# A hybrid decoder step on one Trainium2 core: the sample groups' score and value products, their PSUM banks, and the second layer of the cache compression

## The chip, the cores and the metric

The kernel runs on one core of one Trainium2 chip, as one launch. The metric is the device time of that core in microseconds. TensorE multiplies matrices into PSUM banks of 512 float32 columns; VectorE, ScalarE and GpSimd work beside it; SyncE and GpSimd issue most of the DMAs.

## The reference, cut to what matters

One inference step of a two-layer decoder, for a prompt of 512 tokens and for 8 samples of one token, each with a cache of 2048 positions in 16 pages. The change lies in the sparse attention of the samples:

```python
h = jax.nn.gelu(h_a[:, :-1] + h_b[:, 1:] + h_pe)      # compression, first layer
kc, vc = h @ w2                                        # second layer, for keys and for values
kc = partial_rope(kc, c_end)                           # rotates the first 16 of 64 key dims
p_c = masked_softmax(q . kc);  o_c = p_c @ vc          # compressed branch
_, idx = lax.top_k(importance(p_c), 16)                # 16 of 33 blocks of 64 positions
o_s = softmax(q . ks[idx]) @ vs[idx]                   # selected branch
o_w = softmax(q . kw) @ vw                             # last 512 positions
o = g0 * o_c + g1 * o_s + g2 * o_w
```

## The kernel before, in words

Every layer runs a feed-forward network, a mixer (`mid`) and another feed-forward network; the changed lines are in `mid`. There the 8 samples' compressed cache is computed by one generator (`compress_cache`, samples b = 0 to 7), and the attention of the samples by four others (`samples`, groups g = 0 to 3 of two samples each). `weave` takes the instructions of both by turns; group 3 is woven with the prompt's attention instead. The program is then put in order by a planner, which goes by priorities in the order of the text and by its own costs: when the next instruction of an engine is not ready by its reckoning, a later one that is ready goes first. On the chip each engine follows the order so found, and waits where something is late.

A bank is taken with `bank(pool)`. The pools are opened with `reuse_waits="tile"`: a tile's first writer waits until the readers of the bank's earlier tile are done. The pools are `saM` (one bank, `M`: a group's small products), `saS` (two banks: scores `S` and outputs `O`), `saT` (transposes), `ctp` (one bank, `pa`: second layer of the compression).

The group's products have few rows. A group's 128 rows are four quarters of 32 (two halves z of the cache, two samples j), and each quarter is a product of its own with 32 columns of weights that writes its own 32 partitions. L1189 makes the selected scores, two banks of 512 columns, four quarters each; the pages stand in `G[z, j]`, four tiles of 1 MB from the pool `sag` (four buffers), of which GpSimd gathers three pages each (L1118) and SyncE loads five (L1122). L1198 and L1199 make the window scores and the scores of the sample's own key, L1249 and L1258 the values of the selected pages and of the window, L1262 and L1263 the values of the sample's own row (8 rows of weights), L1264 the compressed branch (127 rows). `fetch_sel` for the group after stands behind L1249, so its DMAs wait for the buffers that L1249 reads. A float32 product shows in the trace as two weight loads and two matmuls (two passes), so counts there are twice those of the text.

In the compression, L708 makes the first layer (with the high and low parts of input and weights), `prepare` (L693 on ScalarE, L694 on VectorE) its inputs a step ahead, L730 the gelu, and `second` the second layer: the keys twice, with `w2` and with its rotated copy `w2r` (L736, and L738 for the prompt in sample 0), the values at L740, then the rotation on VectorE (L742 to L744) and a copy on ScalarE (L745). VectorE's L1192 adds the mask to the scores; the mask comes from the small products L1149 to L1178.

Of the kernel before, what the change touches and what calls it, by code (L numbers as in the profile page):

```python
# [7 lines left out]
F32 = mybir.dt.float32  # L8
# [3 lines left out]
OP = mybir.AluOpType  # L12
# [110 lines left out]
class Trunk:  # L123
# [376 lines left out]
    def mid(self, l):  # L500
        nc, I = self.nc, self.I
# [3 lines left out]
        a = self.pool(att, "att", side="right")  # L505
# [10 lines left out]
        self.w2 = a.tile([128, 2, 64], F32, name="w2")  # L516
        self.w2r = a.tile([128, 64], F32, name="w2r")
        self.hpe = a.tile([128, 2], F32, name="hpe")
# [125 lines left out]
    def compress_start(self, l, p):  # L644

        nc, I = self.nc, self.I
        self.w1 = []
        pet = p.tile([128, 2, 2, 8], F32, name="pet")
        for i in range(2):
            raw = self.rawp.tile([128, 8, 256], F32, name="raw")  # L650
            w = raw.rearrange("p k (z h) -> p (k z) h", h=128)
            nc.sync.dma_start(w, I[("nsa_phi_k1", "nsa_phi_v1")[i]][l].rearrange("(q p) h -> p q h", p=128))
            nc.sync.dma_start(self.w2[:, i], I[("nsa_phi_k2", "nsa_phi_v2")[i]][l])
            nc.sync.dma_start(pet[:, i], I[("nsa_pe_k", "nsa_pe_v")[i]][l].rearrange("p (z q) -> p z q", z=2))
            self.lo = nc.gpsimd
            with self.tc.issue_after(self.queries.ins):
                self.w1.append([self.split(w[:, 8 * z:8 * z + 8]) for z in range(2)])
            self.lo = nc.vector
        nc.vector.memset(self.w2r, 0.0)
        nc.vector.tensor_scalar(self.w2r[:, 0:8], self.w2[:, 0, 8:16], -1.0, None, op0=OP.mult)  # L660
        nc.vector.tensor_copy(self.w2r[:, 8:16], self.w2[:, 0, 0:8])
        return p, pet

    def compress_cache(self, l, p, kcv, cx, G, start):

        nc = self.nc
# [45 lines left out]
        def second(b, acc):  # L712
# [6 lines left out]
            hp = []  # L719
# [12 lines left out]
            pa = self.bank(self.ctp)  # L732
            for j, w in enumerate((self.w2[:, 0], self.w2r)):
                for kv in range(2):
                    r = slice(kv * 64, kv * 64 + 64)
                    nc.tensor.matmul(pa[r, j * 128:j * 128 + 128], w, h[:, kv, :], start=True, stop=True)  # L736
                    if b == 0:
                        nc.tensor.matmul(pa[r, 384 + j * 32:416 + j * 32], w, hp[0][:, 0, kv], start=True, stop=True)  # L738
            for kv in range(2):
                nc.tensor.matmul(pa[:, 256 + kv * 64:256 + kv * 64 + 64], h[:, 2 + kv, :], self.w2[:, 1], start=True, stop=True)  # L740
            t = p.tile([128, 128], F32, name="kct")
            nc.vector.tensor_mul(t, pa[:, 128:256], self.C["kc_sin"])  # L742
            nc.vector.tensor_mul(kcT, pa[:, :128], self.C["kc_cos"])
            nc.vector.tensor_add(kcT, kcT, t)  # L744
            nc.scalar.activation(vc, pa[:, 256:384], AF.Copy)  # L745
            if b == 0:
                t = p0.tile([128, 32], F32, name="pt1")
                nc.vector.tensor_mul(t, pa[:, 416:448], self.C["kc_sin"][:, :32])
                nc.gpsimd.memset(self.kcp, 0.0)
                for kv in range(2):  # L750
                    r = slice(kv * 64, kv * 64 + 64)
                    nc.vector.tensor_mul(self.kcp[r, kv], pa[r, 384:416], self.C["kc_cos"][r, :32])
                    nc.vector.tensor_add(self.kcp[r, kv], self.kcp[r, kv], t[r])
# [370 lines left out]
    def fetch_win(self, l, pw, g):  # L1124
        for j in range(2):
            w = pw.tile([128, 1024], F32, name="W")
            self.nc.sync.dma_start(w, self.I["winT"][l, 2 * g + j])
            self.sgq[g]["w", j] = w

    def samples(self, l, g, p, pg, pw):  # L1130

        nc = self.nc
        G = self.sgq[g]
        QB, kcT, vc = self.QB, self.kcT, self.vc
        M = self.bank(self.saM)

# [49 lines left out]
        for c in range(2):  # L1186
            S = self.bank(self.saS)
            for z, j, r in quarters:
# [4 lines left out]
                                    msk[:, 8 * c:8 * c + 8, None].to_broadcast([128, 8, 64]), op=OP.add)  # L1193
        S = self.bank(self.saS)
        for j in range(2):
            for z in range(2):
                r = 64 * z + 32 * j
                nc.tensor.matmul(S[r:r + 32, :256], QB[:, 2 * g + j], G["w", j][:, 256 * z:256 * z + 256], start=True, stop=True)  # L1198
            nc.tensor.matmul(S[32 * j:32 * j + 32, 256:258], QB[:, 2 * g + j], self.kTs[:, :, 2 * g + j], start=True, stop=True)  # L1199
# [45 lines left out]

        O = self.bank(self.saS)
        for c in range(8):
# [12 lines left out]
        for j in range(2):  # L1260
            own, o = slice(32 * j, 32 * j + 32), slice(64 + 32 * j, 96 + 32 * j)
            nc.tensor.matmul(O[own, :128], sT[:, own], self.srows[:, 128:256], start=False, stop=True, skip_group_check=True)  # L1262
            nc.tensor.matmul(O[own, 128:256], sT[:, o], self.srows[:, 384:512], start=False, stop=True, skip_group_check=True)  # L1263
            nc.tensor.matmul(O[own, 256:384], pc[:, own], vc[:127, j], start=False, stop=True, skip_group_check=True)  # L1264
        yield 900.0
        if g < 3:
# [688 lines left out]
```

## Time and profile before

| | us |
|---|---|
| median of 3 runs (lowest, highest) | 3108.46 (3104.69, 3116.01) |
| the profiled execution, by the device | 3104.94 |
| its span from first to last instruction | 3103.2 |
| TensorE busy, share of the span | 3028.1, 98% |
| VectorE busy | 1598.7, 52% |
| ScalarE busy | 1120.1, 36% |
| GpSimd busy | 536.1, 17% |
| mean granted TensorE clock | 0.987 of full |

Busy times overlap; a matmul's time includes its way through the array, so neighbours overlap as well, and the distance from one start to the next is what counts for TensorE. In timelines, a line is a run of equal instructions (their number behind the x), its start, its length, and in brackets the idle time of the engine before it with what ended it.

### The profile page before, as it was taken

To read this page: it belongs to the slowest core of one execution; us is meant where nothing else is said; L and a number is where in the kernel's file an instruction comes from. 1 tells how busy PE (TensorE), PEld (TensorE's weight loads), DVE (VectorE), ACT (ScalarE), POOL (GpSimd) and SP (SyncE) were. 2 spreads that over 40 slices of the span, in tenths; PEclk is the share of its full clock that TensorE was granted. 3 is DMA by queue.
4 is the path that set the end of the run, shared out by engine and by line. 5 is a ranking of instruction groups with operands and counts; after the bars stand their busy time and mean duration, and the time that the engine had idled before them with its cause. 6 is when DMAs were issued, how large, how long until landed. Compare 5 with 4: busy or idle time off the path is not lost. (4 is left out here: it accounts for less than half of the span.)

```text
span 3103.2 us, 62136 instructions
## 1 busy us (share of the span) xinstructions
PE 3028.1 (98%) x25364; PEld 2906.8 (94%) x25364; DVE 1598.7 (52%) x3586; ACT 1120.1 (36%) x2226; POOL 536.1 (17%) x809
## 2 busy tenths in 40 slices
PE   8999999999999999999999999999999999999998
PEld 8999998777999999999999999887789999999998
DVE  7633356566655365333496333565666453743334
ACT  4332235456224233232233222354652242333322
POOL 2611031321001021001147010213210010210010
PEclk9999999999999999999999999999999999999999
DMA  5543254632553232232234332547234433223221
GB/s 159 198 148 133 89 159 134 209 96 63 156 138 103 88 101 91 82 99 86 82 121 169 96 103 76 172 124 218 83 93 140 122 98 102 89 82 103 89 87 64
DMA packets 358630, 360.17 MB, mean 116 GB/s; under 512 B 40068, under 2 KB 341668, under 8 KB 358216
## 3 DMA queue, kind: packets, MB, share of 16 engines
q1 hardware_dynamic: 342584, 333.58, 34.4%
q0 software_dynamic: 7440, 20.00, 2.2%
q8 instruction: 199, 3.26, 0.4%
q10 hardware_dynamic: 8320, 2.62, 0.4%
q14 instruction: 87, 0.71, 0.1%
HBM read 332.48 MB, written 36.28 MB: 119 GB/s over the span
## 5 line engine op out<-in xcount | busy, mean ns | idle before, releaser
L239 PE MATMUL ps<-xh,whi 128*128 128x264 f32 (+1 forms) x4448 | 1257.6, 285 | 14.1 <-ACT whi L228 6.1
L240 PE MATMUL ps<-xl,whi 128*128 128x264 f32 (+1 forms) x4448 | 1257.4, 284 | 2.0 <-DVE xl L323 2.0
L241 PE MATMUL ps<-xh,wlo 128*128 128x264 f32 (+1 forms) x4448 | 1254.1, 283 | 2.4 <-DVE wlo L229 2.4
L229 DVE TENSOR_TENSOR wlo<-raw,whi 128x1024 fp32r<-128x1024 f32 (+3 forms) x432 | 496.0, 1151 | 741.2 <-ACT whi L228 736.9
L239 PEld LDWEIGHTS ps<-xh,whi 128*128 128x128 f32 x4448 | 837.2, 189 | 18.7 <-ACT whi L228 6.9
L240 PEld LDWEIGHTS ps<-xl,whi 128*128 128x128 f32 x4448 | 839.5, 189 | 3.5 <-DVE xl L323 2.2
L241 PEld LDWEIGHTS ps<-xh,wlo 128*128 128x128 f32 x4448 | 838.5, 189 | 4.1 <-DVE wlo L229 3.6
L228 ACT ACTIVATE whi<-raw 128x1024 fp32r<-128x1024 f32 (+2 forms) x452 | 444.6, 988 | 891.0 <-PE ps L240 776.4
L240 PE MATMUL ps<-hl,whi 128*128 128x256 f32 (+1 forms) x1408 | 398.3, 283 | 0.0
L239 PE MATMUL ps<-hh,whi 128*128 128x256 f32 (+1 forms) x1408 | 398.2, 283 | 0.0
L241 PE MATMUL ps<-hh,wlo 128*128 128x256 f32 (+1 forms) x1408 | 398.1, 283 | 0.0
L241 PEld LDWEIGHTS ps<-hh,wlo 128*128 128x128 f32 x1408 | 265.3, 188 | 0.2
L239 PEld LDWEIGHTS ps<-hh,whi 128*128 128x128 f32 x1408 | 264.9, 188 | 0.3
L240 PEld LDWEIGHTS ps<-hl,whi 128*128 128x128 f32 x1408 | 264.8, 188 | 0.1
L260 POOL TENSOR_TENSOR xf<-xf,shift 128x264 f32<-128x264 f32 (+1 forms) x84 | 79.4, 983 | 1028.6 <-ACT shift L257 1028.6
L384 DVE TENSOR_TENSOR s<-s,ps 128x264 f32<-128x264 f32 (+1 forms) x176 | 74.3, 424 | 277.3 <-PE ps L241 277.0
L708 PE MATMUL ps<-xc,whi 128*128 128x256 f32 (+1 forms) x1024 | 167.4, 297 | 1.0 <-ACT xc L693 0.9
L385 ACT ACTIVATE hh<-s 128x264 fp32r<-128x264 f32 (+1 forms) x176 | 72.7, 415 | 245.2 <-DVE s L384 245.1
L708 PEld LDWEIGHTS ps<-xc,whi 128*128 128x128 f32 x1024 | 142.2, 193 | 14.6 <-issue 7.7
L1118 POOL DMA_INDIRECT sg<-in_selT_dram,idx x96 | 96.2, 1002 | 275.9 <-PE ps L1249 248.7
L382 ACT ACTIVATE s<-ps 128x264 f32<-128x264 f32 (+1 forms) x176 | 66.3, 379 | 128.7 <-PE ps L241 126.5
L386 DVE TENSOR_TENSOR hl<-s,hh 128x264 fp32r<-128x264 f32 (+1 forms) x176 | 76.5, 436 | 33.5 <-ACT hh L385 33.5
(471 smaller groups left out, 4206.8 us busy)
## 6 DMA issues: line engine op xcount, KB each, us to landing
raw<-in_ffn_w_gu_dram SPq DMA_DIRECT2D x86, 1024.0 KB, 5.3
raw<-in_w_in_dram SPq DMA_DIRECT2D x38, 1024.0 KB, 5.4
raw<-in_ffn_w_down_dram SPq DMA_DIRECT2D x32, 1024.0 KB, 4.9
sg<-in_selT_dram SPq DMA_DIRECT2D x160, 128.0 KB, 3.1
cx<-in_cmpT_dram SPq DMA_DIRECT2D x128, 128.0 KB, 2.2
raw<-in_cmpT_dram SPq DMA_DIRECT2D x128, 128.0 KB, 2.5
raw<-in_ffn_w_down_dram SPq DMA_DIRECT2D x16, 768.0 KB, 4.3
W<-in_winT_dram SPq DMA_DIRECT2D x16, 512.0 KB
```

The lines of the kernel that those rows point to most:

```text
L228: self.copy = self.nc.scalar.activation(hi, raw, AF.Copy)
L229: self.lo.tensor_sub(lo, raw, hi.bitcast(F32))
L239: nc.tensor.matmul(o, hi[:, k], rh, start=start and k == 0, stop=False)
L240: nc.tensor.matmul(o, hi[:, k], rl, start=False, stop=False)
L241: nc.tensor.matmul(o, lo[:, k], rh, start=False, stop=stop and k == nk - 1)
L260: nc.gpsimd.tensor_sub(self.xf[:, g, a:b], self.xf[:, g, a:b], sc[:, :n])
L382: nc.scalar.activation(s[:, :n], g, AF.Silu)
L384: nc.vector.tensor_mul(s[:, :n], s[:, :n], u)
L385: nc.scalar.activation(hh[:, j, a:b], s[:, :n], AF.Copy)
L386: nc.vector.tensor_sub(hl[:, j, a:b], s[:, :n], hh[:, j, a:b].bitcast(F32))
L708: nc.tensor.matmul(o, w[:, 2 * qq + q2, :], x[:, 2 * q2:2 * q2 + 2, z:z + n], start=not b and s < 2 and q2 + z + m == 0, stop=s > 5 and q2 ...
L1118: nc.gpsimd.indirect_dma_start(out=t[:, k], out_offset=None, in_=flat, in_offset=bass.IndirectOffsetOnAxis(ap=self.idx[:, l, b, z, k:k + 1 ...
```

## The change

Three parts. `opened` takes a bank and has VectorE write zero into its first column; `samples` uses it for `M`, the three score banks and `O`. In the window scores all four quarters come ahead of the own-key rows; at the end of a group the compressed branch comes first, then the two own-row products, with the two samples j by turns. In the compression `w2` and its rotated copy become one operand `w2k` of 128 columns, so that one product over 256 columns gives the keys of both heads, plain in partitions 0 to 63 and rotated in 64 to 127; the rotation on VectorE then takes four products of 64 partitions instead of two of 128.

```diff
--- before.py
+++ after.py
@@ -514,7 +514,7 @@
         self.kcp = a.tile([128, 2, 32], F32, name="kcp")
         self.vcp = a.tile([128, 4, 2, 64], F32, name="vcp")
         self.w2 = a.tile([128, 2, 64], F32, name="w2")
-        self.w2r = a.tile([128, 64], F32, name="w2r")
+        self.w2k = a.tile([128, 128], F32, name="w2k")
         self.hpe = a.tile([128, 2], F32, name="hpe")
         kcv, sag = self.pool(att, "kcv", 2, side="right"), self.pool(att, "sag", 4, side="right")
         sw = self.pool(att, "sw", 2, side="right")
@@ -656,9 +656,10 @@
             with self.tc.issue_after(self.queries.ins):
                 self.w1.append([self.split(w[:, 8 * z:8 * z + 8]) for z in range(2)])
             self.lo = nc.vector
-        nc.vector.memset(self.w2r, 0.0)
-        nc.vector.tensor_scalar(self.w2r[:, 0:8], self.w2[:, 0, 8:16], -1.0, None, op0=OP.mult)
-        nc.vector.tensor_copy(self.w2r[:, 8:16], self.w2[:, 0, 0:8])
+        nc.vector.memset(self.w2k[:, 64:], 0.0)
+        nc.vector.tensor_copy(self.w2k[:, 0:64], self.w2[:, 0])
+        nc.vector.tensor_scalar(self.w2k[:, 64:72], self.w2[:, 0, 8:16], -1.0, None, op0=OP.mult)
+        nc.vector.tensor_copy(self.w2k[:, 72:80], self.w2[:, 0, 0:8])
         return p, pet
 
     def compress_cache(self, l, p, kcv, cx, G, start):
@@ -730,26 +731,26 @@
                 nc.scalar.activation(h[:, 2 * i:2 * i + 2, :127], hv[:, :, :127], AF.Gelu_apprx_tanh, bias=self.hpe[:, i:i + 1])
             yield 0.0
             pa = self.bank(self.ctp)
-            for j, w in enumerate((self.w2[:, 0], self.w2r)):
-                for kv in range(2):
-                    r = slice(kv * 64, kv * 64 + 64)
-                    nc.tensor.matmul(pa[r, j * 128:j * 128 + 128], w, h[:, kv, :], start=True, stop=True)
-                    if b == 0:
-                        nc.tensor.matmul(pa[r, 384 + j * 32:416 + j * 32], w, hp[0][:, 0, kv], start=True, stop=True)
+
+            nc.tensor.matmul(pa[:, :256].rearrange("p (k n) -> p k n", k=2), self.w2k, h[:, 0:2, :], start=True, stop=True)
             for kv in range(2):
                 nc.tensor.matmul(pa[:, 256 + kv * 64:256 + kv * 64 + 64], h[:, 2 + kv, :], self.w2[:, 1], start=True, stop=True)
+            if b == 0:
+                nc.tensor.matmul(pa[:, 384:448].rearrange("p (k n) -> p k n", k=2), self.w2k, hp[0][:, 0], start=True, stop=True)
             t = p.tile([128, 128], F32, name="kct")
-            nc.vector.tensor_mul(t, pa[:, 128:256], self.C["kc_sin"])
-            nc.vector.tensor_mul(kcT, pa[:, :128], self.C["kc_cos"])
+            for kv in range(2):
+                r = slice(kv * 64, kv * 64 + 64)
+                nc.vector.tensor_mul(t[r], pa[64:128, kv * 128:kv * 128 + 128], self.C["kc_sin"][r])
+                nc.vector.tensor_mul(kcT[r], pa[0:64, kv * 128:kv * 128 + 128], self.C["kc_cos"][r])
             nc.vector.tensor_add(kcT, kcT, t)
             nc.scalar.activation(vc, pa[:, 256:384], AF.Copy)
             if b == 0:
                 t = p0.tile([128, 32], F32, name="pt1")
-                nc.vector.tensor_mul(t, pa[:, 416:448], self.C["kc_sin"][:, :32])
                 nc.gpsimd.memset(self.kcp, 0.0)
                 for kv in range(2):
                     r = slice(kv * 64, kv * 64 + 64)
-                    nc.vector.tensor_mul(self.kcp[r, kv], pa[r, 384:416], self.C["kc_cos"][r, :32])
+                    nc.vector.tensor_mul(t[r], pa[64:128, 384 + kv * 32:416 + kv * 32], self.C["kc_sin"][r, :32])
+                    nc.vector.tensor_mul(self.kcp[r, kv], pa[0:64, 384 + kv * 32:416 + kv * 32], self.C["kc_cos"][r, :32])
                     nc.vector.tensor_add(self.kcp[r, kv], self.kcp[r, kv], t[r])
                 pv = self.bank(self.saM)
                 nc.tensor.matmul(pv[:, :64], hp[1].rearrange("p r k n -> p (r k n)"), self.w2[:, 1], start=True, stop=True)
@@ -1127,12 +1128,18 @@
             self.nc.sync.dma_start(w, self.I["winT"][l, 2 * g + j])
             self.sgq[g]["w", j] = w
 
+    def opened(self, pool):
+
+        b = self.bank(pool)
+        self.nc.vector.memset(b[:, 0:1], 0.0)
+        return b
+
     def samples(self, l, g, p, pg, pw):
 
         nc = self.nc
         G = self.sgq[g]
         QB, kcT, vc = self.QB, self.kcT, self.vc
-        M = self.bank(self.saM)
+        M = self.opened(self.saM)
 
         for j in range(2):
             nc.tensor.matmul(M[32 * j:32 * j + 32, :127], QB[:, 2 * g + j], kcT[:, j, :127], start=True, stop=True)
@@ -1184,18 +1191,17 @@
         nc.vector.memset(SB[64:128, 0::1281], BIG)
         quarters = [(z, j, slice(64 * z + 32 * j, 64 * z + 32 * j + 32)) for z in range(2) for j in range(2)]
         for c in range(2):
-            S = self.bank(self.saS)
+            S = self.opened(self.saS)
             for z, j, r in quarters:
                 nc.tensor.matmul(S[r].rearrange("p (n t) -> p n t", n=4), QB[:, 2 * g + j], G[z, j][:, 4 * c:4 * c + 4, 0:128],
                                  start=True, stop=True)
             yield 2200.0, 0.0
             nc.vector.tensor_tensor(SB[:, 1 + 512 * c:513 + 512 * c].rearrange("p (n t) -> p n t", n=8), S.rearrange("p (n t) -> p n t", n=8),
                                     msk[:, 8 * c:8 * c + 8, None].to_broadcast([128, 8, 64]), op=OP.add)
-        S = self.bank(self.saS)
+        S = self.opened(self.saS)
+        for z, j, r in quarters:
+            nc.tensor.matmul(S[r, :256], QB[:, 2 * g + j], G["w", j][:, 256 * z:256 * z + 256], start=True, stop=True)
         for j in range(2):
-            for z in range(2):
-                r = 64 * z + 32 * j
-                nc.tensor.matmul(S[r:r + 32, :256], QB[:, 2 * g + j], G["w", j][:, 256 * z:256 * z + 256], start=True, stop=True)
             nc.tensor.matmul(S[32 * j:32 * j + 32, 256:258], QB[:, 2 * g + j], self.kTs[:, :, 2 * g + j], start=True, stop=True)
         yield 1800.0
         nc.scalar.activation(SB[:, 1025:1281], S[:, :256], AF.Copy)
@@ -1243,7 +1249,7 @@
         nc.vector.tensor_mul(cf, cf, self.gat[:, g, 1:3])
         yield 300.0
 
-        O = self.bank(self.saS)
+        O = self.opened(self.saS)
         for c in range(8):
             for z, j, r in quarters:
                 nc.tensor.matmul(O[r, :128], PT[:, c, r], G[z, j][:, c, 128:256], start=c == 0, stop=z == 1 and c == 7,
@@ -1258,10 +1264,13 @@
                 nc.tensor.matmul(O[r, 128:256], PT[:, 8 + c, r], G["w", j][:, v:v + 128], start=False, stop=z == 1 and c == 1,
                                  skip_group_check=True)
         for j in range(2):
-            own, o = slice(32 * j, 32 * j + 32), slice(64 + 32 * j, 96 + 32 * j)
-            nc.tensor.matmul(O[own, :128], sT[:, own], self.srows[:, 128:256], start=False, stop=True, skip_group_check=True)
-            nc.tensor.matmul(O[own, 128:256], sT[:, o], self.srows[:, 384:512], start=False, stop=True, skip_group_check=True)
+            own = slice(32 * j, 32 * j + 32)
             nc.tensor.matmul(O[own, 256:384], pc[:, own], vc[:127, j], start=False, stop=True, skip_group_check=True)
+        for br in range(2):
+            for j in range(2):
+                own, o = (slice(k + 32 * j, k + 32 * j + 32) for k in (0, 64 * br))
+                nc.tensor.matmul(O[own, 128 * br:128 * br + 128], sT[:, o], self.srows[:, 256 * br + 128:256 * br + 256], start=False,
+                                 stop=True, skip_group_check=True)
         yield 900.0
         if g < 3:
             self.fetch_win(l, pw, g + 1)
```

## Rows read from the trace of the kernel before

**Rows 1.** The page, part 1: busy us (share of the span) and instructions.

```profile
PE 3028.1 (98%) x25364; PEld 2906.8 (94%) x25364; DVE 1598.7 (52%) x3586; ACT 1120.1 (36%) x2226; POOL 536.1 (17%) x809
```

**Rows 2.** Windows: stretch, us, busy us (count) of PE, PEld, DVE, ACT, POOL, clock, DMA, GB/s.

```profile
574.20:576.05 1.85, 0.00 (x0) 0.00 (x0) 0.00 (x0) 0.00 (x0) 0.00 (x0) 1.00 0.98 330
...
625.70:629.76 4.06, 2.21 (x25) 1.44 (x24) 2.95 (x8) 3.27 (x7) 0.00 (x0) 1.00 0.74 220
629.76:636.58 6.82, 5.96 (x26) 5.65 (x27) 3.50 (x13) 4.15 (x8) 0.00 (x0) 0.50 0.00 0
```

**Rows 3.** Timeline of TensorE, scores of group 1, layer 0 (start, us, line, tile, form, count).

```profile
571.57 1.05 PE L1189 MATMUL ps<-sg,QB 128*32 128x512 f32 x2
572.55 0.38 PE L1149 MATMUL ps<-cst,scp 64*127 64x4 f32 x2
...
573.02 1.05 PE L1189 MATMUL ps<-sg,QB 128*32 128x512 f32 x4
576.09 1.14 PE L1189 MATMUL ps<-sg,QB 128*32 128x512 f32 x4 [2.02 <-DMA raw<-in_cmpT_dram]
```

**Rows 4.** Timeline of TensorE, scores of group 3, layer 0.

```profile
672.02 1.92 PE L1189 MATMUL ps<-sg,QB 128*32 128x512 f32 x16
```

**Rows 5.** Timeline of TensorE, end of group 0, layer 0.

```profile
556.42 0.64 PE L1258 MATMUL ps<-W,PT 128*32 128x128 f32 x16
556.99 0.40 PE L1262 MATMUL ps<-srows,sT 8*32 8x128 f32 x2
...
558.76 0.75 PE L708 MATMUL ps<-xc,whi 128*128 128x256 f32 x4
```

**Rows 6.** Timeline of TensorE, selected values of group 1, layer 0.

```profile
593.56 0.41 PE L1249 MATMUL ps<-sg,PT 128*32 128x128 f32 x2
593.90 0.74 PE L708 MATMUL ps<-xc,whi 128*128 128x256 f32 x4
...
595.53 1.07 PE L1249 MATMUL ps<-sg,PT 128*32 128x128 f32 x30
```

**Rows 7.** Timeline of TensorE and ScalarE, scores of group 0 and the second layer.

```profile
509.81 1.92 PE L1189 MATMUL ps<-sg,QB 128*32 128x512 f32 x14
...
510.66 0.47 ACT L730 ACTIVATE hc<-ps,hpe 128x254 f32<-128x254 f32 x1
...
511.66 0.45 PE L736 MATMUL ps<-hc,w 128*64 128x128 f32 x4
```

**Rows 8.** Timeline of GpSimd, the gathers for group 1, layer 0 (first and last of twelve).

```profile
555.11 0.97 POOL L1118 DMA_INDIRECT sg<-in_selT_dram,idx  x1 [65.93 <-PE ps L1249]
...
569.32 1.19 POOL L1118 DMA_INDIRECT sg<-in_selT_dram,idx  x1 [0.30 <-issue]
```

**Rows 9.** Timeline of VectorE and TensorE, mask addition and window scores of group 2.

```profile
626.69 1.29 DVE L1192 TENSOR_TENSOR SB<-ps,msk 128x512 f32<-128x512 f32 x2
...
627.48 0.65 PE L1198 MATMUL ps<-W,QB 128*32 128x256 f32 x8 [1.57 <-issue]
```

**Rows 10.** Timeline of TensorE, second layer of sample 1, and transposes of group 0.

```profile
526.47 0.44 PE L736 MATMUL ps<-hc,w 128*64 128x128 f32 x4
...
527.06 0.66 PE L740 MATMUL ps<-w,hc 128*128 128x64 f32 x4
...
551.19 1.10 PE L1229 MATMUL ps<-cst,SB 128*128 128x128 f32 x8
552.12 0.28 PE L1236 MATMUL ps<-mx,cst 128*128 128x2 f32 x2
```

**Rows 11.** Timeline of VectorE and ScalarE: a memset, the key rotation, the copy behind it.

```profile
578.06 0.06 DVE L1162 MEMSET score<- 33x4 f32 x1
...
587.95 0.28 DVE L1211 COPY nm<-ps 2x128 f32<-2x128 f32 x1
588.16 0.27 DVE L742 TENSOR_TENSOR kct<-ps,cst 128x128 f32<-128x128 f32 x1
...
588.85 0.28 ACT L745 ACTIVATE vc<-ps 128x128 f32<-128x128 f32 x1 [0.29 <-DVE kcT L743]
```

## The prediction, made before the change was built

> **What bounds the kernel now.** I read the page first. TensorE is busy for 98% of the span [rows 1], so the question for any edit is whether it shortens what TensorE has to do, and whether anything else then holds the place. The change touches one stretch of each layer, the weave of cache compression with the sample groups (490 to 700 us in layer 0, 2032 to 2240 in layer 1), so next I read that stretch by windows. There TensorE is not always the bound. Between 574.20 and 576.05 no engine does anything, and the DMA engines are at 0.98 of their time with 330 GB/s [rows 2]: TensorE stands for a gathered cache page, and the chip can't bring it sooner. Then I read TensorE's own timeline in that place. In group 1 the eight score products of the first half (four quarters, each a float32 product of two passes) come in three pieces: two passes at 571.57, four at 573.02, then a stand of 2.02 us, and the last two with the next half's first two at 576.09 [rows 3]. In group 3, where nothing else was ready, all sixteen passes are one run of 1.92 us [rows 4]. The reader is to see that four quarters side by side cost what one costs alone, and that a quarter sent ahead alone (always the first one of a fresh bank) pays the whole run for itself.
>
> Why the first goes alone: only the first writer of a tile waits for its bank, the other three are ordered behind it, so in the planner's reckoning they are ready later than the first, and other work of higher priority slips in between. A one-column memset as the first writer makes all four ready together. That is what I take the new helper to do.
>
> **Part by part.** All prices are from the profiled execution, 3104.94 us (3103.2 of span and 1.74 around it).
>
> *Single rows at the end of a group.* Before, from 556.99 to the next compression product at 558.76, six products follow each other, 1.77 us, and with each change between 8 and 127 rows the next start comes later; none of the two rows j overlaps the other [rows 5]. The sixteen window passes ahead of them take 0.57 us from 556.42 for four packs of four, one change of form included; a pass alone followed by such a change takes 0.34 [rows 5, 6]. So a pack is about 0.11 and a change about 0.20. Afterwards the pair over `vc` needs no change behind the window products (two packs, 0.22), then one change (0.20), four packs of the two other products (0.44), and one change back, instead of four changes and no packing: some 0.95 against 1.97 counted from the last window pack, 1.0 us less. That is eight times, but see the next but one part for where it lies.
>
> *Score quarters.* A lone first quarter costs about 1.0 us (571.57 to 572.55) [rows 3]. There are four such, groups 1 and 2 in both layers. In group 0 of each layer two passes went ahead, and fourteen passes run from 509.81 until the second layer starts at 511.66; with eight left they end about 0.85 earlier, but the hidden rows come from ScalarE only at 510.66 + 0.47 = 511.13 [rows 7], so 0.45 is gained, 0.9 for two layers.
>
> *What the stand does with these.* The pages of group g+1 are asked for when the last selected-value product of group g is done: the first gather starts at 555.11, the twelfth at 569.32, one every 1.29 us, and the data of the last quarter let TensorE go at 576.09, 21.0 us after the first [rows 3, 8]. GpSimd's issue and the DMA engines set that distance, not TensorE. All that TensorE saves between those two points lengthens the stand and gains nothing: the end rows of groups 0 and 1, the lone quarters of groups 1 and 2, and the second layer of samples 3 and 5. One of the four places (layer 0, group 2) shows no such stand, but 1.57 us idle at 627.48 a little later [rows 9]; I count it as absorbed too. The end rows of groups 2 and 3 lie behind the last gather that is waited for: 4 x 1.0 = 4.0 us on the path. Bounds for this part: nothing absorbed, 4 x 1.0 more from the end rows and 4 x 1.0 from the quarters; or the pack of four, now inseparable, goes in front of the mask products (L1149 to L1158), so that these come after the landing instead of in front of it, 1.0 us lost at each of four places. I take 0.
>
> *Value quarters.* In groups 1 and 2 one pair of passes goes alone at 593.56, and the rest, thirty, follow at 595.53 [rows 6]. The pair costs 0.34 and some 0.06 of entering the form; the thirty are eight packs as thirty-two would be, so their 1.07 us stay. This lies behind the landing and in front of the next request, so it counts: 4 x 0.4 = 1.6. In group 3 the runs are cut up by prompt attention; 0, at most 0.6 a layer.
>
> *Second key layer as one operand.* Eight passes of 128 x 64 take 0.59 us (526.47 to 527.06) [rows 10]. Two passes over 256 columns are not in the trace; the nearest row is eight transposes of 128 columns in 0.93 us (551.19 to where the next line starts, 1.10 with the last one's end), 0.116 each [rows 10], so 0.23 a pass, 0.46 in all, and about 0.1 for the change of form that falls away: 0.25 us a sample. From below it is 0.12 (the entry is hidden), from above 0.4. Samples 4 and 6 wait for the hidden rows in any case, 3 and 5 lie in front of the stand; per layer 0.3 for sample 0 (with its prompt columns), 0.25, 0.1 and 0.1 for samples 1, 2 and 7: 1.5 us in all. Upper end 16 x 0.25 = 4.0.
>
> *What is added.* VectorE gets 40 memsets; the nearest row has 0.06 us, a small copy 0.28 [rows 11]: 2.4 to 11 us of an engine that is busy for half the time. The memset of the third score bank must stand behind both mask additions on VectorE (626.69, two in 1.29 us), while today the window scores start when the first of them is done [rows 9]. Behind L1198 on TensorE stands the second layer, on ScalarE the copy L1201 and behind that the second gelu. That is up to 0.65 + 0.06 at four places; mostly the second layer waits for its gelu then anyway; I take 0.2 each, 0.8 (0 to 2.9). The key rotation has four products instead of two on VectorE; a row starts 0.21 after the one before it and lasts 0.27 [rows 11], so 0.4 us a sample, 6.7 in all, and ScalarE's copy of `vc` waits as much longer (it waits 0.29 now). Compression products are prepared a step ahead, which covers it; cost 0.5 in all (0 to 6.7). If that cover were gone, the whole 0.4 would show at each of sixteen samples.
>
> [...]
>
> **Sum.** 4.0 + 0.9 + 1.6 + 1.5 - 0.8 - 0.5 = 6.7 us less: 3098.2 for an execution like the profiled one. The median of the three runs shown is 3108.46, 3.5 above it (the lowest is 3104.69). I put half of that on: 3100 us.
>
> **Rivals.**
> *The stand gives way.* If the planner fills the stand with compression products, or the gathers land sooner because they are asked for sooner, all of TensorE's savings count: 8.0 + 4.0 + 1.7 + 1.6 + 4.0 - 1.3 = 18 us, 3087 + 2 = 3089. For it: one of four places shows no stand at this line. Against it: 330 GB/s and the 1.29 us per gather in the other three.
>
> *The pack stands for its last page, and the clock falls.* The four quarters go as one, TensorE stands in front of the mask products, and its stand grows from 2 us to over 4 (1.0 + 1.0 + 0.25 longer). [...] Three such places are new: 3 x 3.4 + 4 x 1.0 = 14.2 on top of the sum: 3114, slower than before. It decides from the second fall of the clock on. For it: the savings are right in front of the stand. Against it: the planner, not I, sets the place of the pack. [...]
>
> *The quarters stay apart.* If what parts them is that their pages land at different times in the planner's reckoning, and not the bank, the memsets change nothing: without 0.9 and 1.6 the sum is 4.2, 3102.5. For it: four tiles, four landings. Against it: the lone one is the first in the value products too, whose pages have long landed.
>
> **How the numbers follow.** Forecast 0.52 (its own range 3095 to 3106, from the costs of what is added and the placing of the stand); the stand gives way 0.20; the clock falls 0.18; the quarters stay apart 0.10. 8 of 10 lie between 3087 and 3114: the lower end is the second case, the upper one the third. Half a percent is 15.5 us, about what a measurement of this kernel tells from no change, so faster means under 3093: nearly all of the second case and a little of the first, 0.23; slower means over 3124: 0.07, a third of the clock case; the rest, 0.70, within.
>
> **What would show it.** Right: in the trace after, L1189 comes in runs of eight or sixteen with no pair ahead of them; the value products in 32 or 64; the end rows take about 0.75 instead of 1.77 us; the second layer has two passes with 256 columns; and TensorE's idle time in front of the score products of groups 1 and 2 is longer by about 2 us with the same 21 us from first gather to landing. Wrong: the stand is not longer and the time falls by over 15 us, or PEclk shows new stretches of 0.50 in 555 to 645 or 2098 to 2185.

## The result and the profile after: slower by 0.9%

The changed kernel takes 3136.76 us (median of 4 runs, 3133.26 to 3138.02) against 3106.57 (4 runs, 3101.03 to 3116.01): ratio 1.0092, 95% interval 1.0072 to 1.0112. Forecast were 3100 us, with a range of 3087 to 3114.

The page of the changed kernel, span, part 1 and one line of part 2, to be held against [rows 1]:

```profile
span 3136.3 us, 61978 instructions
PE 3041.2 (97%) x25256; PEld 2919.5 (93%) x25256; DVE 1612.6 (51%) x3662; ACT 1118.8 (36%) x2226; POOL 539.3 (17%) x809
...
PEclk9999999989999999999999999999899999999999
```

TensorE issues 108 fewer matmuls and is busy for 13 us more. Its work is done more slowly: the mean granted clock is 0.979 against 0.987. The clock is granted at one of two levels in these traces, full (1.00 in the rows) and half (0.50); a change from full to half is called a fall below. Six passes of the scores take 0.99 us to the next start at 1.00 (2119.53 in the kernel before) and 1.86 at 0.50 (582.99 in the changed one). If the rest ran at full clock, the means say 2 x 0.021 x 3136 = 132 us at half clock after and 2 x 0.013 x 3103 = 81 before (136 and 83 where the windows of 0.50 are added up, 2 us of each behind the last instruction). Half of the 53 us more is 26.5 of the 33.1 us between the two spans, if TensorE worked all through them. Of the 53, some 38 are in the changed stretch; the rest is in falls at places where the code is as before, and such falls differ between two executions of one kernel too (table below).

Windows of the changed kernel (columns as in [rows 2]): the stand of group 1 in layer 0, then the stretches of `mid` that were granted half clock in layer 0, then those in layer 1.

```profile
578.41:581.33 2.92, 0.01 (x2) 0.04 (x2) 0.00 (x0) 0.00 (x0) 0.00 (x0) 1.00 0.95 329
582.40:585.80 3.40, 3.40 (x19) 1.67 (x19) 1.73 (x8) 0.00 (x0) 0.00 (x0) 0.50 0.88 284
626.80:630.20 3.40, 3.26 (x15) 0.98 (x18) 0.47 (x4) 0.00 (x0) 0.00 (x0) 0.50 1.05 367
660.90:667.70 6.80, 5.36 (x22) 4.64 (x22) 4.17 (x14) 3.27 (x8) 5.28 (x6) 0.50 0.84 257
667.70:674.50 6.80, 6.30 (x34) 5.50 (x35) 4.12 (x21) 3.22 (x16) 0.06 (x1) 0.50 0.63 222
695.00:701.80 6.80, 5.13 (x26) 4.64 (x25) 5.55 (x16) 3.02 (x9) 1.27 (x1) 0.50 0.01 2
```

```profile
2138.90:2142.30 3.40, 3.40 (x19) 1.67 (x20) 1.71 (x8) 0.00 (x0) 0.00 (x0) 0.50 0.73 235
2183.20:2190.00 6.80, 5.95 (x25) 2.59 (x26) 1.72 (x8) 0.00 (x0) 0.00 (x0) 0.50 0.81 261
2220.80:2234.40 13.60, 12.03 (x60) 9.91 (x60) 8.38 (x39) 6.80 (x25) 4.12 (x5) 0.50 0.67 225
2254.90:2261.70 6.80, 4.72 (x22) 4.53 (x22) 3.87 (x12) 3.31 (x11) 0.82 (x1) 0.50 0.00 0
```

There are three kinds of place in each layer. In or behind the stands at the pages of groups 1 and 2 the clock falls four times, 17 us in all (before: once, 6.8 us, [rows 2]). At the start of group 3 it falls for 13.6 us in each layer; half of that was there in the kernel before:

```profile
660.50:667.30 6.80, 6.65 (x35) 5.83 (x35) 3.71 (x20) 2.75 (x10) 0.65 (x1) 0.50 0.71 250
667.30:674.10 6.80, 6.67 (x59) 4.09 (x58) 3.70 (x15) 2.83 (x12) 1.84 (x2) 1.00 0.00 0
```

And in the prompt's attention woven with group 3 (695.00 and 2254.90) both falls are new.

TensorE's timeline in the changed kernel, scores of group 1 in layer 0 (against [rows 3]):

```profile
575.91 1.04 PE L1196 MATMUL ps<-sg,QB 128*32 128x512 f32 x2
576.89 0.38 PE L1156 MATMUL ps<-cst,scp 64*127 64x4 f32 x2
...
577.36 1.05 PE L1196 MATMUL ps<-sg,QB 128*32 128x512 f32 x4
581.33 1.15 PE L1196 MATMUL ps<-sg,QB 128*32 128x512 f32 x4 [2.91 <-DMA sg<-in_selT_dram,idx]
```

The pair of passes still goes alone, then four, then a stand, 2.9 instead of 2.0 us: the memset did not join the quarters.

### The profile page after: what moved, and what is told of

Its sections match the earlier page's. It is cut to its first block, busy times and chain, and to the rows that moved or that the text cites. A ratio compares the mean times of both kernels' runs of the same rounds, so it can differ in the third digit from the quotient of the medians.

```text
span 3136.3 us, 61978 instructions
## 1 busy us (share of the span) xinstructions
PE 3041.2 (97%) x25256; PEld 2919.5 (93%) x25256; DVE 1612.6 (51%) x3662; ACT 1118.8 (36%) x2226; POOL 539.3 (17%) x809
## 5 line engine op out<-in xcount | busy, mean ns | idle before, releaser
L239 PEld LDWEIGHTS ps<-xh,whi 128*128 128x128 f32 x4448 | 839.6, 190 | 21.1 <-ACT whi L228 8.9
L709 PEld LDWEIGHTS ps<-xc,whi 128*128 128x128 f32 x1024 | 142.9, 193 | 20.6 <-issue 10.1
```

Source lines behind the costliest of these rows:

```text
L239: nc.tensor.matmul(o, hi[:, k], rh, start=start and k == 0, stop=False)
L709: nc.tensor.matmul(o, w[:, 2 * qq + q2, :], x[:, 2 * q2:2 * q2 + 2, z:z + n], start=not b and s < 2 and q2 + z + m == 0, stop=s > 5 and q2 ...
```

## Experiments

Four theories. A: the memsets put VectorE in front of TensorE. B: the longer key rotation delays VectorE's and ScalarE's work for TensorE. C: whatever TensorE saves in front of the gathered pages lengthens its stand, and the clock falls behind it. D: C's stands are chance, or the rows have a cost of their own.

The experiments were measured in five sets, with the kernel before in each. In two of them the kernel before took 3106 and 3107 us, as in the profile shown (*early pages* below). In the other three it took 3195 to 3201 us itself (*late pages*), with another stand. So each ratio is against the kernel before of its own set, with its 95% interval behind it.

### One part at a time (early pages)

Rows alone: quarters first in the window scores, end rows by turns, nothing else. The order on all other engines is that of the kernel before.

```diff
-        for j in range(2):
-            (sT x srows), (sT x srows), (pc x vc)   of row j
+        for j in range(2): (pc x vc)
+        for br in range(2):
+            for j in range(2): (sT x srows) of branch br
```

> Only the order of the single rows changes (quarters first in the window scores, end rows by turns). Theory A (what costs is the banks' memset on VectorE in front of TensorE's first product): rows alone are faster, the eight groups' end rows by 1.0 us each, 4 to 8 us less than before. Theory B (what costs is the key rotation on VectorE and ScalarE's copy behind it): the same, 4 to 8 us less. Theory C (any shortening of TensorE's work in front of the gathered pages lengthens the stand there and lets the clock fall): 5 to 15 us more than before, with new stretches of PEclk 0.50 behind groups 1 and 2.

Measured: 3118.02 us, ratio 1.0030 (1.0019 to 1.0041): C's side, 10.6 us more where A and B have 4 to 8 less. The end rows save what was forecast; the stands that follow are longer, and the clock falls in or behind them. TensorE's timeline, then windows, of the rows alone (four of the windows are those of the four stands):

```profile
571.06 1.05 PE L1189 MATMUL ps<-sg,QB 128*32 128x512 f32 x2
...
577.87 2.01 PE L1189 MATMUL ps<-sg,QB 128*32 128x512 f32 x4 [4.31 <-DMA sg<-in_selT_dram,idx]
...
652.67 0.65 PE L1257 MATMUL ps<-W,PT 128*32 128x128 f32 x16
653.14 0.39 PE L1261 MATMUL ps<-vc,pc 127*32 127x128 f32 x4
653.46 0.63 PE L1265 MATMUL ps<-srows,sT 8*32 8x128 f32 x8
654.01 0.74 PE L708 MATMUL ps<-xc,whi 128*128 128x256 f32 x4
...
660.41 0.44 PE L736 MATMUL ps<-hc,w 128*64 128x128 f32 x4 [1.41 <-ACT hc L730]
```

```profile
573.56:577.87 4.31, 0.00 (x1) 0.04 (x2) 0.00 (x0) 0.00 (x0) 0.00 (x0) 0.78 1.01 352
576.00:582.80 6.80, 4.93 (x20) 1.57 (x21) 1.71 (x8) 0.00 (x0) 0.00 (x0) 0.50 0.80 263
661.30:668.10 6.80, 5.45 (x26) 4.51 (x24) 4.02 (x20) 3.83 (x13) 4.28 (x5) 0.50 0.86 255
668.10:674.90 6.80, 6.80 (x36) 5.84 (x37) 3.67 (x18) 2.75 (x10) 0.00 (x0) 0.50 0.53 182
...
623.80:630.60 6.80, 4.77 (x20) 1.38 (x21) 1.71 (x8) 0.00 (x0) 0.00 (x0) 0.50 0.79 251
2122.20:2129.00 6.80, 4.70 (x19) 1.31 (x20) 1.71 (x8) 0.00 (x0) 0.00 (x0) 0.50 0.76 241
2170.00:2173.40 3.40, 3.04 (x15) 1.03 (x18) 0.29 (x1) 0.00 (x0) 0.00 (x0) 0.50 0.88 288
```

The end rows take 0.87 us, 653.14 to 654.01, against 1.77 [rows 5]. Only part of the longer stand is the saved microsecond: counted from the first gather the pages also landed later than in the execution before (22.3 us against 21.0 in group 1 of layer 0), which may be chance of the execution.

The traces of this part settle most of that. Each has four places where TensorE can stand for the pages, groups 1 and 2 in two layers. In the four traces with the new order of the rows (rows, the two of rows and key layer, the change) it stands at all sixteen, 1.86 to 4.40 us, 3.1 on average, and in or behind each the clock falls. In the four without it (before, memsets, key layer, rotation of five) it stands 0 to 2.83 us, 1.3 on average, and the clock falls at three of these stands (1.79, 2.37 and 2.83 us). In the whole change the last page lands 20.3 us after the first gather on average, as before (20.4), and the stands are 2.5 us against 1.1: there the saved time lengthens them, not the landing. In the rows alone it lands after 21.7 us, so there the landing adds to it. D's chance alone does not make sixteen of sixteen.

The banks' memsets alone (all five), and the second key layer with its rotation alone:

```diff
-        S = self.bank(self.saS)        (M, S twice, window S, O)
+        S = self.opened(self.saS)
```

> Only the memset of one column at the opening of the five banks of a group. Theory A: most of the loss is here, 20 to 30 us more than before, with TensorE standing for the memset of the bank M at the start of group 3 and the clock falling behind it. Theory B: within 5 us of before. Theory C: within 5 us of before, since no product of TensorE is shortened.

Measured: 3121.40 us, 1.0051 (1.0038 to 1.0064). More than B and C allow, less than A wanted. The order changes on VectorE, ScalarE and TensorE. The largest single place that I found is not the memset in front of TensorE but the prompt's softmax: TensorE's timeline, then the window before the fall and that of the fall,

```profile
685.76 0.22 PE L1244 MATMUL ps<-cst,ex 64*8 64x64 f32 x1 [0.75 <-DVE ex L1227]
...
688.05 0.33 PE L1050 MATMUL ps<-masks,identb 128*128 128x128 bf16 x1
690.21 0.69 PE L1025 MATMUL ps<-cst,cP 128*128 128x128 f32 x2 [1.82 <-DVE cP L1021]
```

```profile
679.70:686.50 6.80, 5.72 (x38) 4.17 (x37) 4.72 (x15) 6.34 (x20) 1.04 (x1) 1.00 0.00 1
686.50:693.30 6.80, 4.97 (x24) 4.49 (x24) 5.32 (x16) 2.79 (x9) 1.27 (x1) 0.50 0.00 0
```

and the same in layer 1, and twice in the whole change (695.00, 2254.90 above), but not with the rows or the key layer alone. The clock falls at 686.50, ahead of the wait for `cP` (688.39 to 690.21), so that wait did not bring it down (nor did it at 2236.10 here and at 695.00 in the whole change, where the fall is ahead as well); in front of the fall stand shorter waits, for `ex` among them, and TensorE is busy for 5.72 of 6.80 us. That these bring the fall is not shown.

```diff
-   (4 products of 64 columns, w2 and w2r; 2 + 1 on VectorE)
+   matmul(pa[:, :256], self.w2k, h[:, 0:2, :])
+   for kv: t[r] = pa[64:128] * sin; kcT[r] = pa[0:64] * cos
```

> Only the second key layer as one operand of 128 columns with its rotation from partitions 64 and 0 by turns. Theory A: 1 to 4 us less than before. Theory B: most of the loss is here, 20 to 30 us more, with the products of the rotation some 0.30 us apart, ScalarE's copy of vc behind them, and group 3 with prompt attention 8 us longer in each layer. Theory C: 5 to 15 us more, since two passes take the place of eight.

Measured: 3119.43 us, 1.0039 (1.0026 to 1.0052): 12 us more, in C's 5 to 15, without A's gain and without B's 20 to 30. TensorE's timeline shows VectorE late twice in each layer (here layer 0):

```profile
523.33 1.24 PE L709 MATMUL ps<-xc,whi 128*128 128x256 f32 x8 [0.72 <-DVE xc L695]
...
554.58 0.38 PE L1221 MATMUL ps<-cst,nm 2*128 2x2 f32 x2 [0.60 <-DVE nm L1219]
```

Neither wait is there before.

The change without the memsets (its edit is the first and the third above), in both sets with early pages:

> The change without the memsets at the opening of the banks. Theory A: 5 to 12 us less than before. Theory B: the loss stays, 20 to 28 us more than before. Theory C: 10 to 25 us more than before.

> The change without the memsets at the opening of the banks, beside the kernel before. On a chip where before takes about 3200 us (the rows alone: ratio 0.999, the whole change: 1.005): theory B (the second key layer's rotation on VectorE carries what is left of the loss): ratio 1.003 to 1.005; theory A (the memsets carry it): 0.998 to 1.001. Where before takes 3107 us: 1.004 as it was.

Measured: 3118.24 us, 1.0039 (1.0025 to 1.0052), and 3122.58 us, 1.0057 (1.0044 to 1.0069). That is 10.9 and 16.8 us more. A, as the cause of all, falls, B's 20 to 28 is missed, and both lie in C's 10 to 25; the second is above the 1.004 that was expected of it. Against 1.0092 for the whole, the memsets carry some 11 to 16 us.

Only VectorE's extra work, in the kernel before (TensorE's as it was):

```diff
+            for _ in range(2):
                 nc.vector.tensor_mul(t, pa[:, 128:256], self.C["kc_sin"])
                 nc.vector.tensor_mul(kcT, pa[:, :128], self.C["kc_cos"])
```

> The kernel before with both products of the key rotation issued twice, so that VectorE has five instructions per sample and TensorE's work is unchanged. Where before takes about 3200 us, theory B: ratio 1.002 to 1.004 (up to 0.4 us at each of sixteen samples, 6.7 us, and the first layer's inputs on VectorE behind them); theory A or a cost on TensorE's side: 0.999 to 1.001. Where before takes 3107 us: theory B 1.002 to 1.004 as well, with the waits of the first layer for xc as in the run of the second key layer alone.

Measured: 3110.82 us, 1.0014 (1.0003 to 1.0026): 4.4 us, a third of what the key layer costs; below B's 0.002, above A's 0.001. TensorE's waits in it from 515 to 560 us, largest first (us in total, times, longest); the kernel before has one such wait in this stretch, 0.2 us:

```profile
PE ps L1139 <- DVE vcp L760: 0.7, 1, 0.7
PE ps L1179 <- DVE mk L1175: 0.2, 1, 0.2
PE ps L1215 <- DVE nm L1213: 0.2, 1, 0.2
PE ps L708 <- DVE xc L694: 0.2, 1, 0.2
```

The profiles of these runs, split as above: half-clock time added up from windows of 0.50 (2.0 us of each row lie behind the last instruction); its cost over the kernel before at one half; what is left of the longer span; and, added up over 455 to 740 and 2000 to 2300 us, TensorE's waits for VectorE and for DMAs:

| run | span | clock | us at half clock | cost | left | waits for VectorE | waits for DMAs |
|---|---|---|---|---|---|---|---|
| before | 3103.2 | 0.987 | 82.7 | | | 11.3 | 4.4 |
| rows | 3114.3 | 0.982 | 113.5 | 15.4 | -4.3 | 11.5 | 15.0 |
| memsets | 3115.6 | 0.985 | 93.1 | 5.2 | 7.2 | 17.0 | 6.3 |
| key layer | 3119.6 | 0.985 | 96.0 | 6.7 | 9.7 | 16.4 | 5.7 |
| rows and key layer | 3115.8 | 0.984 | 102.8 | 10.1 | 2.5 | 15.6 | 11.0 |
| the same, second set | 3121.4 | 0.982 | 112.2 | 14.8 | 3.4 | 15.6 | 13.3 |
| rotation of five | 3108.5 | 0.987 | 85.3 | 1.3 | 4.0 | 13.2 | 3.4 |
| the change | 3136.3 | 0.979 | 135.8 | 26.6 | 6.5 | 21.1 | 10.0 |

One execution each, and falls outside the stretch come and go (the two executions of rows and key layer are 9.4 us apart at half clock): a row is good to some 5 us. The cost column is an upper bound where TensorE stood at half clock. The last two columns part the mechanisms: the rows add waits for DMAs and hardly any for VectorE, while the memsets and the key layer add 5.7 and 5.1 us of waits for VectorE, most of what is left for the one and half of it for the other.

### Meant for C, measured with late pages

End rows by turns in groups 2 and 3 alone (`if g >= 2:` around the new order, the old one else; the window scores have their new order in all groups):

> The single rows' new order, the end rows by turns in groups 2 and 3 alone; groups 0 and 1, which stand in front of the gathered pages, keep their old end. Theory C (the time saved in front of a gather lengthens TensorE's stand, and the clock falls behind it): the new falls behind groups 1 and 2 (6.8, 6.8 and 3.4 us at half clock with the rows everywhere) do not come; the 1 us saved in group 2 still lengthens the wait at the start of group 3, whose fall stays at 13.7 us: 3105 to 3110, against 3118 with the rows everywhere. Theory D (the pages landed late by chance or because of the DMA engines, whatever the rows do): 3113 to 3120, with stands over 4 us in group 1 as well.

> The end rows by turns in groups 2 and 3 alone, once more, since in the run before the kernel before itself took 3196 us, with TensorE waiting 12 us in every group for an input page of the compression. If the kernel before takes about 3107 us here: theory C, no new falls behind groups 1 and 2, 0 to 4 us less than before (3103 to 3108; up to 7 more if the fall at the start of group 3 is 13.7 us as with the rows everywhere). Theory D, the landing of the pages varies by itself: stands over 4 us in group 1 here too, 3113 to 3120.

> The end rows by turns in groups 2 and 3 alone. Where before takes about 3107 us: theory C, ratio 0.998 to 1.001, below the rows everywhere by 7 us or more. Theory D: ratio 1.002 to 1.004. Where it takes 3200 us: 0.998 to 0.999 by both.

Measured: 3193.20, 3197.87 and 3192.03 us, ratios 0.9981 (0.9969 to 0.9993), 0.9986 (0.9975 to 0.9996), 0.9987 (0.9976 to 0.9998). With late pages these part C from D in nothing.

The rows everywhere, and the whole change, in the third of these sets:

> The rows' new order in all groups, as in the first of these runs, now beside the others on one chip. If the kernel before takes about 3107 us here (TensorE stands for the gathered pages in groups 1 and 2): theory C, 7 to 13 us more than before, as then. If it takes about 3200 us (TensorE stands for an input page of the compression and not for the gathered pages): theory C, 4 to 9 us less than before, ratio 0.997 to 0.999, since there is no stand at the pages that the saved time could lengthen. Theory D (the rows cost by something of their own): 7 to 13 us more on either.

> The whole change beside the others on one chip. Where before takes about 3107 us: ratio 1.008 to 1.011, as it was. Where it takes 3200 us: theory C, ratio 1.000 to 1.005, since the falls behind the stands at the pages have no place there; theories A and B, 1.007 to 1.010, since the memsets and the rotation cost the same wherever the pages land.

Measured: rows 3191.65 us, 0.9988 (0.9977 to 0.9999), C's side of the fork; the change 3211.42 us, 1.0047 (1.0031 to 1.0062), in C's range, at its upper end.

Here the rows make the kernel *faster*, by 3 to 4 us, the 4.0 of the sum, and hardly more in all groups than in the late two. What stands is shown by ScalarE, VectorE, TensorE and SyncE (rows alone, this set):

```profile
582.45 1.15 ACT L693 ACTIVATE xc<-cx 128x512 fp32r<-128x512 f32 x2 [15.45 <-remote]
...
582.36 0.35 DVE L1271 TENSOR_SCALAR OS<-ps,cf 128x128 f32<-128x128 f32 x1 [14.77 <-remote]
...
583.53 0.69 PE L1275 MATMUL ps<-cst,OS 128*128 128x64 f32 x2 [4.37 <-DVE OS L1273]
...
548.92 9.53 SPq L641 DMA_DIRECT2D cx<-in_cmpT_dram  x16
565.09 21.35 SPq L1122 DMA_DIRECT2D sg<-in_selT_dram  x20
```

TensorE is idle for some 10 us at group 1 and again at group 2, not the 12 of the expectations, and nothing is left of the stand at the gathered pages. That it waits for an input page of the compression, as the expectations say, is not shown: ScalarE's next instruction does read one (`cx`), but its loads were issued by 558.5, and VectorE, whose next instruction reads none, stands until the same 582.4. The profile names no releaser for either (`remote`). The clock falls at these stands in any case: for 13.7 us at each of groups 1 and 2 and 27.3 at group 3 in both layers, with the rows in all groups as with those in the late two. So the contrast with early pages is not between a stand and none, but between one with a new fall behind it and one whose fall is there already.

The same twenty page loads take 14.38 us of SyncE in the kernel before, with early pages:

```profile
554.87 14.38 SPq L1122 DMA_DIRECT2D sg<-in_selT_dram  x20
```

Useless products to fill the stand, in groups 1 and 2 (n = 12) and, in the last three, at sample 7 (8 more into `pa`):

```diff
+            for _ in range(n if c == 0 and g in (1, 2) else 0):
+                nc.tensor.matmul(S[0:32, :128], QB[:, 2 * g], self.C["kc_sin"], start=True, stop=True)
```

> The new order of the rows in all groups, and in groups 1 and 2 twelve useless products of 128 columns (24 passes of some 0.11 us, 2.6 us) in front of the score quarters, in their own bank. They take up part of the stand (3.2 to 5.0 us there with the rows alone). Theory C: the falls behind these groups (6.8, 6.8, 6.8 and 3.4 us) go, about 12 us less than with the rows alone: 3103 to 3109, though TensorE does more. Theory D: the filler costs what it takes or nothing: 3116 to 3128.

> The rows in all groups and twelve useless products in front of the score quarters of groups 1 and 2, once more. Theory C: without the falls behind these groups, about 12 us less than the rows alone, ratio to before 0.998 to 1.001. Theory D: ratio 1.003 to 1.007.

> The rows everywhere and twelve useless products in front of the score quarters of groups 1 and 2. Where before takes about 3107 us: theory C, ratio 0.998 to 1.001, theory D 1.003 to 1.007. Where it takes 3200 us: 1.002 as measured twice, by both, as nothing stands there.

> The whole change, with the same twelve products in groups 1 and 2 and eight more in front of the second layer of sample 7, where group 3 begins and TensorE waits for the gelu. Theory C: the falls behind groups 1 and 2 (17 us in all) go and those of 13.7 us at group 3 come down to 6.8: 12 to 16 us less than the change alone, 3120 to 3125. Theory A (memsets in front of TensorE) and theory B (the rotation): 3130 to 3145, since nothing of either is taken away.

> The whole change with the twenty useless products, once more. Theory C: 12 to 16 us less than the change alone, ratio to before 1.004 to 1.006. Theories A and B: ratio 1.007 to 1.012.

> The kernel before with the same twenty useless products. Theory C: of its falls those behind group 2 of layer 0 and at the start of group 3 (6.8 us each, three of them) can go, 10 us at most, and up to 3 us are lost where nothing stands: 3097 to 3108. Theory D: 3107 to 3118.

Measured: rows and filler 3202.63, 3208.17 and 3204.71 us, ratios 1.0022 (1.0009 to 1.0035), 1.0020 (1.0011 to 1.0030), 1.0025 (1.0013 to 1.0037); the change and filler 3218.05 and 3222.49, 1.0066 (1.0051 to 1.0082) and 1.0059 (1.0042 to 1.0076); the kernel before and filler 3212.57, 1.0049 (1.0033 to 1.0065). With the rows the filler costs 13 us over the rows alone of the same set, about what it takes on TensorE (4 places x 24 passes x 0.11 = 10.6): nothing hides it there. These six say nothing on C, whose stand at the gathered pages was absent.

The memset of M alone:

> The memset at the opening of the bank M alone, of the five banks that the change opens so. Theory A (TensorE's first product of a group waits for VectorE): the larger part of what all five cost (15 us) is here, 8 to 15 us more than before, with the wait of TensorE for the memset in group 3. Rival (the memsets of the score banks and of the outputs cost it, by the order they bring about on VectorE): 0 to 4 us more.

Measured: 3205.56 us, 1.0009 (0.9998 to 1.0020). For the rival, with late pages; A's 8 to 15 us do not come there. With early pages it was not measured.

## Why the prediction was wrong

*The step that failed.* "All that TensorE saves between those two points lengthens the stand and gains nothing": the saving was absorbed, as it says, but the longer stand was priced at nothing ("I take 0"), and the second rival, which prices it by the clock, got 0.18. The rows alone show the step: the stands are longer, and 15.4 us of clock come with them. What is left without the clock is -4.3 us, beside the 4.0 of the sum; they agree no better than the 5 us that a row is good to, and some 6 us of that half clock lie in the stands themselves, where they cost nothing. The same edit gains 3 to 4 us with late pages, where the fall is there with or without it. No run has late rows or a filled stand with early pages. The prediction's own sign of being wrong came: new stretches of 0.50 at 582.40, 2138.90 and 2183.20.

The second rival had the kind and not the sizes. It counted three new falls behind the pages, and three are there; but these places have 17.0 us at half clock against 6.8, which costs 5.1 us and not 3 x 3.4. Its 3.4 is half of the 6.82 us at 0.50 in [rows 2]; no run shown here has it at all three new places: they have 3.4, 3.4 and 6.8 us at half clock in the changed kernel (582.40, 2138.90, 2183.20), and 6.8, 6.8 and 3.4 in the rows alone (576.00, 2122.20, 2170.00). What it and the sum left out costs more: the longer falls at the start of group 3 and the two in the prompt's attention, 13.6 us more at half clock each, 13.6 us of time together. In or behind all four stands of the rows alone (4.3 and 4.4 us in layer 0) the clock is granted at 0.50; three such stands in the kernel before, 1.2 to 2.0 us, have no fall. What brings the clock down at the one and not at the other is not shown.

*What is added* was the second failure: 0.8 us for the memsets and 0.5 for the rotation, with the sum's other terms at their values. Alone they measure 1.0051 for the memsets, about 16 us (bound: 2.9), and 1.0014 for VectorE's part of the rotation (4.4 us, inside its bound of 6.7). The memsets were priced by the wait for each; what they did was to change the planner's order, down to the prompt's softmax, where TensorE now waits 1.7 to 2.6 us for `cP` (0.3 before) and the clock falls. M's memset does hold TensorE once in each layer, at the start of group 3 (VectorE, then TensorE, in the whole change):

```profile
659.06 0.68 DVE L969 TENSOR_TENSOR raw<-qT,raw 64x512 fp32r<-64x512 f32 x1
659.75 0.06 DVE L1134 MEMSET ps<- 128x1 f32 x1
...
663.28 0.29 DVE L743 TENSOR_TENSOR kct<-ps,cst 64x128 f32<-64x128 f32 x1 [1.35 <-PE ps L737]
663.59 0.28 DVE L744 TENSOR_TENSOR kcT<-ps,cst 64x128 f32<-64x128 f32 x1
663.89 0.29 DVE L743 TENSOR_TENSOR kct<-ps,cst 64x128 f32<-64x128 f32 x1
```

```profile
659.96 0.38 PE L1145 MATMUL ps<-kcT,QB 128*32 128x127 f32 x2 [0.82 <-DVE ps L1134]
661.28 1.22 PE L735 MATMUL ps<-hc,w2k 128*128 128x256 f32 x2 [0.94 <-ACT hc L731]
```

*The quarters.* The mechanism was wrong, the third rival right: scores of groups 1 and 2 go 2, 8 and 6 passes as before, values 2 and 30. The 1.6 us of the sum for the values are not there, nor is what the sum wanted of the scores. In the planner's order other products still go between, the mask's in the scores (L1156 above), whoever writes the bank first; that it is the landing of the pages that parts them, the rival's reason, is not shown.

*Sizes that held.* End rows: from the first window product to the next step it is 1.0 us less in each of the eight groups, as forecast (its own terms, 0.22, 0.20, 0.44 and 0.20, add to 1.06 and not to the 0.95 that it gives). Second key layer, from its first pass to the values' first, in the changed kernel:

```profile
529.45 0.60 PE L735 MATMUL ps<-hc,w2k 128*128 128x256 f32 x2
529.88 0.55 PE L737 MATMUL ps<-w,hc 128*128 128x64 f32 x4
```

0.43 us against 0.59 [rows 10], 0.16 saved for the 0.25 taken. Rotation: its products stand 0.31 us apart (663.28 to 663.59), against 0.21 [rows 11]. Each is 0.28 to 0.29 us long and starts when the one before has ended, where the 0.27 us product of [rows 11] starts 0.07 ahead of that; what holds them is not shown.

*Open.* The parts alone add to 1.20%, the whole is 0.92%; whether they share part of their cost is at the edge of the intervals. Two thirds of the key layer's cost are not VectorE's instruction count; the table puts 5.1 us of it on waits for VectorE and 6.7 on the clock, and the rest stays open. Why the clock falls in the prompt's attention, and for how much of the longer fall at the start of group 3 the rows' stand there answers, was not tested. No version measured beats the kernel before with early pages; with late pages the rows do by 0.12%, the late rows by 0.13 to 0.19%.

## What to carry to other kernels

Time saved in front of a transfer that TensorE waits for was not free of effect here (15.4 us of clock with the rows alone, by the table): price the longer stand by the clock behind it, with a row of the same trace on either side, before writing 0. An instruction given to a planner is priced by the order that comes out, on every engine, not by its own microseconds. And run a part alone before judging a change of several: here a pure reordering that saves TensorE 1 us in each group cost 0.3%.

## What the runs showed of the hardware that was not expected

One and the same kernel took 3106 to 3107 us in two sets of runs and 3195 to 3201 in three, and single edits changed sign between them (rows 1.0030 and 0.9988). With late pages the traces show SyncE's twenty loads in 21.4 us instead of 14.4, and ScalarE and VectorE standing for some 15 us until the same moment; why a set is of one kind or the other, and what the engines wait for, they don't show.
